# A hybrid decoder layer on one core: other queue, places and order for its recurrence (S5)

## The chip, the cores and the metric

One core of a Trainium2 chip runs the whole layer as one program. The metric is the device time of one execution in microseconds; the kernel before takes 786.01 us (median of three runs, 784.77 to 787.89).

## The reference

One layer of a decoder for 16 meta tokens and 512 prompt tokens in one sequence, and 8 sequences of 8 new tokens each with 1024 cached ones. The input is projected once to u, c_q, c_kv and k_r. u runs through a complex diagonal state space (S5: 32 groups of 16 channels and 64 states), the rest through latent attention with four heads. Their outputs share a projection, and a convolutional gated FFN follows. Cut to what the change touches:

```python
z = xn @ w_in;  u, c_q, c_kv, k_r = split(z, [512, 896, 1152])
abar, bbar = s5_discretise(a, log_dt, b)             # complex, per group
h[t] = abar * h[t-1] + bbar @ u[t]                   # associative scan over t
y = (re(h) @ c_re - im(h) @ c_im) + d * u
y = gelu(y);  y = y * sigmoid(y @ w_glu)
x = x + concat(y, mla) @ w_out
f = (silu(causal_conv(xn2 @ w_gate)) * (xn2 @ w_up)) @ w_down;  x = x + f
```

All outputs are float32: y, the latent cache rows, the final states and the last convolution rows.

## The kernel before, in words

The 592 tokens stand on the free axis, 128 features on the partitions. A product of two float32 matrices is made of three matmuls: both sides are split into a high part (ScalarE, L393) and a low part (VectorE, L394), and high x high, high x low and low x high are summed in PSUM (`mm3`). Small products of the recurrence run in plain float32, and such a matmul appears as two half passes.

SBUF is a set of banks A to J, one tile each; `R.get(name, shape, type, bank, at)` gives a place in a bank and `R.put` gives it back. The framework adds all waits from the accesses to those places, and plans the order of each engine's instructions from a timeline of its own: ready instructions in order of priority, which is the order in which the code emits them, moved forward by the numbers `p_...` and `f_...` of `KN` for the parts so named. Generators ("flows") yield amounts of planned time, so that their parts are emitted between the main line's.

**u and z.** `u_phase` forms u in four blocks (PSUM), scales it by `rxb` into `us`, both in bank D, stores each block to DRAM (`ud`, L638) and loads it back with the groups on other partitions (`U`, L639), all on SyncE's queue. `z_phase` forms c_q in three blocks; its evacuation copies the high part into `cqh`, at the beginning of bank D (as float32r, another type, so that the whole bank has to be free), takes the low part, and squares into `zacc` and `ztmp` (L675 to L676); GpSimd sums the squares (L678). Weights come through a ring of three buffers (`fill`, L237); the three blocks of c_kv's weights (`b_kv`) use that ring too.

**The recurrence.** Eight tokens form a chunk, so 74 chunks stand on the free axis. `w2_flow` prepares the matrices that turn a chunk of u into a state, four quarters in two buffers (VectorE L948 to L953, then transposes on TensorE). `taps_flow` prepares the chunk's own kernel: VectorE L1003 to L1008 fill `d3`, matmuls make the taps, and SyncE stores them as `kd` (L1020). Behind both, matmuls of W2 and U give the states `hb`, and eleven steps and a last one of four VectorE instructions each (`add_scaled`, L902 to L906) scan them over the chunks. In `hb` and `d3` the two groups of a pair lie on the two halves of the partitions, with real and imaginary part side by side. `swap` (three ScalarE copies of 64 partitions) exchanges halves, in `d3` for each quarter and in `hb` once, so that afterwards one group's real and imaginary parts fill 128 partitions.

**The output.** `s5_out_flow` loads T from `kd` (eight DMAs a quarter, L1046, two places in bank E for four quarters), and for each quarter and each parity runs a batch of four groups: T times U, then `d3` times `hb`, added in one PSUM bank (tag `bg`, one buffer). A copy to Y, a store (`yd`, L1066), four loads back (`ys`, L1073) and one gelu over all (L1075) follow. `glu` splits the result and multiplies it by the gate's weights. The flow starts at step 2 of `prompt_attn`, whose steps are 20 units of head and token block; the attention of the sampled tokens, the output projection and the FFN come behind the gate.

Names on the timelines are those of the banks: `bankD<-mmp` at L389 is the copy into `cqh`, `ud<-bankD` the store of u, `bgp` the PSUM bank of the recurrence, `krs` and `kr` the rotated keys, of which some matmuls use only 64 partitions.

Of the kernel before, what the change touches and what calls it, by code (L numbers as in the profile page):

```python
# [10 lines left out]
F32 = mybir.dt.float32  # L11
F32R = mybir.dt.float32r
I32 = mybir.dt.int32
AF = mybir.ActivationFunctionType
# [3 lines left out]
ADD, SUB, MUL = ALU.add, ALU.subtract, ALU.mult  # L18
AX = mybir.AxisListType.X

D = 1024
# [3 lines left out]
NT = NP + NS  # L25
S5W = 512
G = 32
P5 = 64
H5 = 16
# [10 lines left out]
LC = 8  # L40
NCP = NP // LC
NC = NT // LC
# [100 lines left out]
def dap(ap, off, dims):  # L143
# [4 lines left out]
KN = dict(bgb=1, chunks=(4, 6, 6, 6), cpo='0P1g2Wu34', cvo=0, endt=18.0, f_exp=24, f_s5=40, f_taps=28, gd=16,  # L148
          gdep=(2, 3), gord=(0, 1, 2, 3, 4), keyx=0, kre='pvvvp', lag=4, ldo='0P1g2W34W', mmb=4,
          order=(4, 3, 1, 2, 0), outs=2, outy=0.01, p_absorb=121, p_finT=-57, p_frows=126, p_inner2=243,  # L150
          p_innerT=-14, p_keys=26, p_pv=-261, p_qmm=25, p_qrope=-19, p_ropek=-199, p_scan=519, p_soft1=-22,
          p_ssoft=21, p_vals=-14, p_w0=98, warm=14, p_w1=78, p_w3=146, pfill=(1, 1, 2, 2, 3, 3), pre=(2, 3), pvd=(1, 1),
          rog='aaav', s2d=1, s5t=40.0, s5y=1.2, sume='pppp', swy=1.0, tapeng='vvvvvvvv',
          tapt=0, tapy=3.0, tpb=3, useng='vvpvppv', valx=4, w2q=((0, 2), (1, 3)), w2s=3.0, w2t=24.0, wsp=(2, 3),
# [139 lines left out]
class K:  # L294
# [124 lines left out]
    def weights(self):  # L419
        A, R, nc, v = self.A, self.R, self.nc, self.nc.vector  # L420
        one = lambda src: (lambda raw: [(raw, src)])
        items = []

        def add(src, shape, **kw):
            items.append(dict(src=src, shape=shape, **kw))

        def kv_split(k0, k1):
            def f(raw):
                self.split(raw, self.wc[:, 0, k0:k1], self.wc[:, 1, k0:k1])
            return f  # L430
        early = {3: ("C", 1024), 4: ("C", 0)}
        for j in range(7):
            add((lambda raw, j=j: [(raw[:, :4], A["b_in"][j][:, :4])]) if j < 2 else one(A["b_in"][j]), [8, 128])
            if j in early:
                items[-1]["at"] = early[j]
        for k0, k1 in ((0, 3), (3, 6), (6, 8)):
            add(one(A["b_kv"][:, k0:k1]), [k1 - k0, 320], split=kv_split(k0, k1))

        for j in range(6):
            add(one(A["b_uq"][j]), [3, 128])  # L440
        add(one(A["b_uk"]), [2, 512])
        add(one(A["b_uv"]), [2, 512])
        for m in range(4):
            add(one(A["b_glu"][m]), [4, 128])
        for m in (*KN["pre"], *range(8)):
            add(one(A["b_out"][m]), [8, 128])
        up = lambda nm, f: add(one(A[nm][f]), [8, 128])
        for c, (f0, f1) in enumerate(self.chunks):
            for f in range(f0, f1):
                if f == f0 == 0 or f > f0:  # L450
                    up("b_gate", f)
                up("b_up", f)
            if f1 < NF:
                up("b_gate", f1)
            for plan in self.plans(f1 == NF):
                self.add_down(add, items, A[f"b_down{c}"], (f1 - f0) // 2, plan)
        return Weights(self, items)
# [46 lines left out]
    def startup(self):  # L504
        nc, A, R, v, cp, p = self.nc, self.A, self.R, self.nc.vector, self.cpool, self.nc.gpsimd
        S = nc.sync
# [42 lines left out]
        ps = self.bg_ps()  # L549
# [2 lines left out]
        self.now = 5.0  # L552
        self.s5 = self.start(self.s5_flow(), pri="f_s5")
        self.step(self.s5)
        jk = R.get("junk", [512], F32, "D", 3472).bitcast(mybir.dt.bfloat16)
        for j in range(2):
            W.parts[j] = tuple(self.wtile(t, [8, 128]) for t in ("wh", "wl"))

# [57 lines left out]
    def u_phase(self):  # L616

        nc, A, R, v, S = self.nc, self.A, self.R, self.nc.vector, self.nc.sync
        W = self.W
        rxb = R.get("rxb", [NT], F32, "D", 2368)  # L620
        us = R.get("us", [4, LC, NC], F32, "D", 0)

        self.ud = self.dram.tile([4, LC, 128, NC], F32, name="ud")
        self.U = R.get("U", [G, NC], F32, "E", 3904)
        pm = self.pm = R.get("p1c", [KVR + 320], F32, "E", 0)
        S.dma_start(pm, A["c_p1"])
        self.gkv = pm[:, :KVR]
        self.rope = pm[:, KVR:].rearrange("p (i j) -> p i j", i=5)
        self.cmask = self.cpool.tile([128, 128], F32, name="cmask")
        self.smask = self.cpool.tile([128, 2, 64], F32, name="smask")  # L630

        def evac(m):
            ps = self.ups.pop(m)
            for o, a, b in UH:
                v.tensor_tensor(us[:, m, ::-1, a // LC:b // LC].rearrange("p s c -> p c s"),
                                ps[:, o, :b - a].rearrange("p (c s) -> p c s", s=LC),
                                rxb[:, a:b].rearrange("p (c s) -> p c s", s=LC), op=MUL)
            S.dma_start(self.ud[m].rearrange("s p c -> p s c"), us[:, m])  # L638
            S.dma_start(self.U[:, 8 * m:8 * m + 8].rearrange("p g c -> p (g c)"),  # L639
                        self.ud[m].rearrange("s (h g) c -> (s h) (g c)", g=8))  # L640
        self.u_part(2, 0, 5)
        pt = self.bg_ps()
        for i in range(4):
            self.T(pt[:, 128 * i:128 * i + 128], self.rx[:, i:i + 1].to_broadcast([128, 128]))
        self.copy(rxb[:, :512], pt)
        pt = self.bg_ps()
        self.T(pt[:, :128], self.rx[:, 4:5].to_broadcast([128, 128]))
        self.copy(rxb[:, 512:], pt[:, :NT - 512])
        W.split()
        self.u_part(2, 5, 8)  # L650
        evac(0)
        self.u_part(3, 0, 8, 0)
        evac(1)
        W.split()
        self.u_part(3, 0, 8, 1)
        evac(2)
        evac(3)
        self.loaded = True
        self.wc = R.get("wc", [2, 8, 320], F32R, "F", 0)
        R.put("us", "rxb")  # L660
# [107 lines left out]
    def s5_flow(self):  # L768
# [65 lines left out]

        b = self.bq
        bb = self.bb = R.get("bb", [2, NG, H5], F32, "E", 576)
        tb = R.get("tb", [2, NG, H5], F32, "D", 2960)
        fb = lambda r: f[:, r, :, None].to_broadcast([128, NG, H5])
        self.cmul(v, (bb[:, 0], bb[:, 1]), (fb(0), fb(1)), (b[:, 0], b[:, 1]), (tb[:, 0], tb[:, 1]))
        R.put("tb", "s5b")  # L840
# [70 lines left out]
            d = 1 << j  # L911
            add_scaled((3 * d, 66, 2 * d), (2 * d, 66 - d, 2 * d), j)
        add_scaled((74, 83, 1), (65, 74, 1), 0)
        self.scanned = True
        yield KN["endt"]
        hc = ts.rearrange("p g x r c -> p (g x r c)")[:, :256].rearrange("p (r b g) -> p r b g", r=2, b=8)
        self.copy(hc, hb[:, :, :, 75:83].rearrange("p g r b -> p r b g"))
# [9 lines left out]
        for r, n in enumerate(("o_re", "o_im")):  # L927
            nc.sync.dma_start(A[n + "_p"][0, 0].rearrange("(G a) p -> G (a p)", a=2), so[:16, 0, r])
            nc.sync.dma_start(A[n + "_s"][0].rearrange("b (G a) p -> (b G) (a p)", a=2), so[:, 1, r])
        yield KN["swy"]  # L930
        self.swap(hb[:, :, 0, :NC], hb[:, :, 1, :NC], ts.rearrange("p g x r c -> p (g x r c)")[:, :NG * NC].rearrange("p (g c) -> p g c", g=NG))
        R.put("scan")
        self.scan_done = True

    def w2_flow(self, eng, qs, at):

# [4 lines left out]
        for q in qs:  # L941
# [10 lines left out]
            eng.tensor_tensor(tmp[:, 1], pb[2], bc[2], op=MUL)  # L952
            self.w2i = eng.tensor_tensor(im, im, tmp[:, 1], op=SUB)  # L953
            yield 0.0
            while "x" in R.used:
                yield 0.5
            if "w2" not in R.used:
                self.w2t = R.get("w2", [4096], F32, "H", 0)
# [12 lines left out]
    def taps_flow(self):  # L971
# [5 lines left out]
        bd = R.get("bd", [2, 4, 2, H5], F32, "J", 0)  # L977
        v.memset(bd, 0.0)
        self.cs = R.get("s5cs", [16, H5], F32, "J", 256)
        v.tensor_tensor(self.cs, ct[:, 0], ct[:, 1], op=ADD)  # L980
        self.kd = self.dram.tile([H5, G, 240], F32, name="kd")
        zt = R.get("ztap", [112], F32, "J", 2240)
        v.memset(zt[:16], 0.0)
# [8 lines left out]
        for q in range(4):  # L992
# [7 lines left out]
            for i in range(2):  # L1000
                e = v if KN["tapeng"][2 * q + i] == "v" else p
                if i == 0:
                    e.tensor_tensor(dim, cb[0], pb[0], op=MUL)  # L1003
                e.tensor_tensor(tmp[:, i], cb[1 + i], pb[1 + i], op=MUL)
                if i == 0:
                    e.tensor_tensor(dre, dim, tmp[:, 0], op=SUB)
                else:
                    e.tensor_tensor(dim, tmp[:, 1], dim, op=SUB)  # L1008
# [10 lines left out]
            v.tensor_tensor(ksb[:, q, :H5], ksb[:, q, :H5], dm[:, q], op=ADD)  # L1019
            nc.sync.dma_start(self.kd.rearrange("h g m -> g h m")[8 * q:8 * q + 8, :, 112:], ksb[:, q])  # L1020
            yield 0.5
            x = tmp.rearrange("p i g k h -> p (i g k h)")[:, :512].rearrange("p (g k h) -> p g k h", g=4, k=8)
            self.swap(dre[:, :, 1:], dim[:, :, 1:], x)
            yield 0.5
        R.put("bd", "s5cs", "ztap", "dm", "ksb", "taptmp", "bb", "ct")
        self.taps_done = True

    def swap(self, a, b, t):

        self.copy(t[:64], b[:64])  # L1030
        self.copy(b[:64], a[64:])
        self.copy(a[64:], t[:64])

    def s5_out_flow(self):

# [6 lines left out]
        def load_T(q):  # L1042
            T[q] = R.get(f"T{q}", [8, LC, H5], F32, "E", 576 + 1024 * (q % 2))
            for s in range(LC):
                b = 16 * (LC - 1 - s)
                S.dma_start(T[q][b:b + 16].rearrange("h g t e -> h g (t e)"), self.kd[:, 8 * q:8 * q + 8, b:b + 128])  # L1046
        load_T(0)
        while not getattr(self, "scan_done", False):
            yield 0.5
# [3 lines left out]
        for q in range(4):  # L1053
            Y = R.get(f"Y{q}", [8, NC], F32, "E", 2624 + 592 * (q % 2))
            for a in range(2):
                ps = self.bg_ps()[:, :4 * NC].rearrange("p (g c) -> p g c", g=4)
                for j in range(4):
                    g = 8 * q + 2 * j + a
                    self.mm(ps[:, j], T[q][:, g % 8].rearrange("p t h -> p (t h)"), U[:, g], True, False)
                    self.mm(ps[:, j], d3[:, a, g // 2, 1:9].rearrange("p t h -> p (t h)"), hb[:, g // 2, a, :NC], False, True)  # L1060
                self.copy(Y[:, a:8:2], ps)
                yield KN["outy"]
            R.put(f"T{q}")
# [6 lines left out]
        ys = R.get("ys", [4, LC, NC], F32, "E", 0)  # L1070
        self.yg = R.get("yg", [4, NT], F32, "E", 2368)
        for m in range(4):
            self.ysd = S.dma_start(ys[:, m], self.yd[m].rearrange("t p c -> p t c"))  # L1073
        yield 8.0
        nc.scalar.activation(self.yg.rearrange("p m (c t) -> p m t c", t=LC), ys, AF.Gelu_apprx_tanh)  # L1075
        R.put("ys")
        self.gelu_done = True

# [920 lines left out]
```

## Time and profile before

| | us |
|---|---|
| median of three runs | 786.01 |
| the profiled execution | 791.1 |
| its span, first to last instruction | 789.3 |

| engine | busy us | share of the span |
|---|---|---|
| TensorE, matmuls (PE) | 742.7 | 94% |
| TensorE, weight loads (PEld) | 690.4 | 87% |
| VectorE (DVE) | 539.1 | 68% |
| ScalarE (ACT) | 351.3 | 45% |
| GpSimd (POOL) | 169.2 | 21% |

The mean granted clock of TensorE is 0.967 of 2.4 GHz. A row of a timeline gives the start and the length of one instruction (or of a run of like ones, x their number), counted from the span's start, and in brackets how long the engine had been idle before it and what ended that. Matmuls overlap in the pipeline, so the length of one is more than its share; the distance between two starts shows the pace. SPq and POOL rows with a DMA are the issue, not the transfer.

### The profile page before, as it was taken

To read this page: it belongs to the slowest core of one execution; us is meant where nothing else is said; L and a number is where in the kernel's file an instruction comes from. 1 tells how busy PE (TensorE), PEld (TensorE's weight loads), DVE (VectorE), ACT (ScalarE), POOL (GpSimd) and SP (SyncE) were. 2 spreads that over 40 slices of the span, in tenths; PEclk is the share of its full clock that TensorE was granted. 3 is DMA by queue.
4 is the path that set the end of the run, shared out by engine and by line. 5 is a ranking of instruction groups with operands and counts; after the bars stand their busy time and mean duration, and the time that the engine had idled before them with its cause. 6 is when DMAs were issued, how large, how long until landed. Compare 5 with 4: busy or idle time off the path is not lost.

```text
span 789.3 us, 14335 instructions
## 1 busy us (share of the span) xinstructions
PE 742.7 (94%) x5594; PEld 690.4 (87%) x5594; DVE 539.1 (68%) x1168; ACT 351.3 (45%) x661; POOL 169.2 (21%) x223
## 2 busy tenths in 40 slices
PE   9979978999879999999999999999999999999985
PEld 8979876778675567999999999999999999999885
DVE  7888999835335333644789566797666996667894
ACT  6435856666473312534334234343333432433643
POOL 0012021000220000331144011551111650114460
PEclk9989999779879999999999999999999999999998
DMA  9890331015694031332223322224222233322203
GB/s 338 239 172 25 97 98 47 6 44 153 197 347 164 1 133 52 108 102 74 67 54 114 121 79 77 61 61 154 66 95 68 61 94 106 99 76 88 52 22 120
DMA packets 41308, 81.49 MB, mean 103 GB/s; under 512 B 13380, under 2 KB 20468, under 8 KB 40216
## 3 DMA queue, kind: packets, MB, share of 16 engines
q1 hardware_dynamic: 39448, 70.09, 29.9%
q0 software_dynamic: 1792, 10.49, 3.6%
q8 instruction: 44, 0.72, 0.4%
q14 instruction: 24, 0.20, 0.1%
HBM read 74.18 MB, written 6.38 MB: 102 GB/s over the span
## 4 chain that ended last, share of the span: by engine, by line
PE 71%; DVE 14%; DMA 7%; ACT 5%; issue 2%; SPq 0%; DVEq 0%; ACTq 0%
PE mmp L379 57%; PE tpp L379 7%; DVE wl L394 4%; PE tpp L385 4%; PE bgp L379 4%; DMA ud<-bankD 1%; DMA bankC<-b_in 1%; DVE bankD L1784 1%; DMA bankF<-xrow 1%; DVE bankA L1736 1%; DMA wraw<-b_down 1%; ACT wh L393 1%; DMA wraw<-b_kv 1%; DMA bankG<-xT 1%; DVE bankC L394 1%
## 5 line engine op out<-in xcount | busy, mean ns | idle before, releaser
L379 PE MATMUL mmp<-bankF,wh 128*128 128x288 f32 (+1 forms) x768 | 224.1, 300 | 7.3 <-ACT bankF L393 7.0
L379 PE MATMUL mmp<-bankF,wl 128*128 128x288 f32 (+1 forms) x736 | 219.6, 299 | 0.2 <-DVE wl L394 0.2
L393 ACT ACTIVATE wh<-wraw 128x1024 fp32r<-128x1024 f32 (+3 forms) x103 | 85.4, 830 | 156.9 <-PE mmp L379 130.7
L379 PEld LDWEIGHTS mmp<-bankF,wh 128*128 128x128 f32 x768 | 146.0, 193 | 7.7 <-ACT bankF L393 7.2
L379 PEld LDWEIGHTS mmp<-bankF,wl 128*128 128x128 f32 x736 | 140.0, 190 | 0.4 <-DVE wl L394 0.4
L394 DVE TENSOR_TENSOR wl<-wraw,wh 128x1024 fp32r<-128x1024 f32 (+3 forms) x103 | 114.3, 1111 | 35.8 <-ACT wh L393 35.5
L379 PE MATMUL mmp<-bankH,wh 128*128 128x288 f32 (+1 forms) x440 | 130.5, 297 | 0.0
L379 PEld LDWEIGHTS mmp<-bankH,wh 128*128 128x128 f32 x440 | 83.7, 190 | 0.0
L379 PE MATMUL mmp<-bankB,wh 128*128 128x288 f32 (+2 forms) x324 | 76.3, 305 | 4.4 <-ACT wh L393 2.2
L379 PE MATMUL mmp<-bankJ,wh 128*128 128x288 f32 (+1 forms) x264 | 78.6, 298 | 0.0
L379 PEld LDWEIGHTS mmp<-bankB,wh 128*128 128x128 f32 x324 | 54.3, 191 | 7.7 <-ACT wh L393 3.1
L379 PE MATMUL mmp<-bankA,wh 128*128 128x290 f32 (+2 forms) x216 | 51.6, 303 | 5.6 <-ACT zacc L676 5.1
L379 PEld LDWEIGHTS mmp<-bankJ,wh 128*128 128x128 f32 x264 | 50.2, 190 | 0.0
L1749 POOL TENSOR_TENSOR bankA<-bankA,bankE 128x576 f32<-128x576 f32 x22 | 27.2, 1235 | 98.6 <-DVE bankA L1746 96.5
L1745 DVE TENSOR_TENSOR bankA<-bankA,mmp 128x288 f32<-128x288 f32 (+1 forms) x44 | 18.2, 420 | 42.8 <-PE mmp L379 28.7
L394 DVE TENSOR_TENSOR wl<-bankE,wh 128x384 fp32r<-128x384 f32 (+1 forms) x66 | 46.0, 715 | 0.0
L379 PE MATMUL mmp<-bankA,wl 128*128 128x290 f32 (+2 forms) x152 | 45.1, 302 | 0.0
L379 PEld LDWEIGHTS mmp<-bankA,wh 128*128 128x128 f32 x216 | 37.2, 192 | 7.0 <-ACT zacc L676 5.4
L393 ACT ACTIVATE wh<-bankE 128x384 fp32r<-128x384 f32 (+1 forms) x66 | 30.3, 486 | 15.1 <-PE mmp L379 5.8
L379 PE MATMUL mmp<-bankB,wl 128*128 128x288 f32 (+1 forms) x118 | 35.3, 299 | 1.6 <-DVE wl L394 1.6
L1738 ACT ACTIVATE bankA<-bankA 128x592 f32<-128x592 f32 x22 | 15.4, 700 | 47.3 <-DVE bankA L1737 47.3
L379 PE MATMUL mmp<-bankG,wh 128*128 128x288 f32 x150 | 34.3, 295 | 0.0
(425 smaller groups left out, 1672.7 us busy)
## 6 DMA issues: line engine op xcount, KB each, us to landing
wraw<-b_gate SPq DMA_DIRECT2D x22, 512.0 KB, 3.4
wraw<-b_up SPq DMA_DIRECT2D x22, 512.0 KB, 3.4
wraw<-b_down SPq DMA_DIRECT2D x17, 384.0 KB, 3.0
wraw<-b_out SPq DMA_DIRECT2D x10, 512.0 KB, 3.6
bankF<-xrow SPq DMA_DIRECT2D x5, 512.0 KB, 7.8
bankA<-b_down SPq DMA_DIRECT2D x6, 384.0 KB, 3.1
bankE<-kd SPq DMA_DIRECT2D x32, 64.0 KB, 2.2
bankG<-xT SPq DMA_DIRECT2D x6, 296.0 KB, 4.8
```

What stands on the lines that cost most here:

```text
L379: self.nc.tensor.matmul(out, lhsT, rhs, start=start, stop=stop, **kw)
L385: self.nc.tensor.transpose(out, src, self.ident[:n, :n])
L393: nc.scalar.activation(hi, src, AF.Copy)
L394: nc.vector.tensor_tensor(lo, src, hi, op=SUB)
L1736: v.scalar_tensor_tensor(c[:, :m], g[:, 1:NG - 1], self.gcol("cw1", f), c[:, :m], op0=MUL, op1=ADD)
L1738: nc.scalar.activation(s[:, :m], c[:, :m], AF.Silu)
L1745: v.tensor_tensor(c[:, a:a + n], s[:, a:a + n], pu[:, o, :n], op=MUL)
L1749: nc.gpsimd.tensor_tensor(c[:, :NU], c[:, :NU], self.rfb[:, 2:], op=MUL)
L1784: v.tensor_tensor(x, ps, x, op=ADD)
```

## The change

c_kv's weights get places of their own in bank H instead of the ring's; `rxb` moves to H, `us` to G (where x was), two small scratch tiles move from D to E, so that bank D holds c_q alone. The loads of U, T and ys are issued by GpSimd instead of SyncE. W2's transposes are emitted behind z, and the taps' VectorE work is ordered behind W2's. `swap` is gone: the output multiplies the real and the imaginary part in two matmuls of 64 partitions each. The output flow gets a priority of 150, no longer waits for the states' store and the exchange to be emitted, and its gelu runs in four blocks.

```diff
-KN = dict(... p_scan=519, p_soft1=-22,
+KN = dict(... p_scan=519, f_out=150, p_soft1=-22,
...
-            add(one(A["b_kv"][:, k0:k1]), [k1 - k0, 320], split=kv_split(k0, k1))
+            add(one(A["b_kv"][:, k0:k1]), [k1 - k0, 320], split=kv_split(k0, k1), at=("H", 592 + 320 * k0))
...
-        jk = R.get("junk", [512], F32, "D", 3472).bitcast(mybir.dt.bfloat16)
+        jk = R.get("junk", [512], F32, "E", 1760).bitcast(mybir.dt.bfloat16)
...
-        rxb = R.get("rxb", [NT], F32, "D", 2368)
-        us = R.get("us", [4, LC, NC], F32, "D", 0)
+        rxb = R.get("rxb", [NT], F32, "H", 0)
+        us = R.get("us", [4, LC, NC], F32, "G", 256)
...
-            S.dma_start(self.U[:, 8 * m:8 * m + 8].rearrange("p g c -> p (g c)"),
+            nc.gpsimd.dma_start(self.U[:, 8 * m:8 * m + 8].rearrange("p g c -> p (g c)"),
...
-        tb = R.get("tb", [2, NG, H5], F32, "D", 2960)
+        tb = R.get("tb", [2, NG, H5], F32, "E", 1760)
...
-        self.scanned = True
+        self.scan_done = True
         yield KN["endt"]
...
-        yield KN["swy"]
-        self.swap(hb[:, :, 0, :NC], hb[:, :, 1, :NC], ts.rearrange("p g x r c -> p (g x r c)")[:, :NG * NC].rearrange("p (g c) -> p g c", g=NG))
         R.put("scan")
-        self.scan_done = True
...
-            while "x" in R.used:
+            while "x" in R.used or not hasattr(self, "fq"):
...
-        v.tensor_tensor(self.cs, ct[:, 0], ct[:, 1], op=ADD)
+        self.after(v.tensor_tensor(self.cs, ct[:, 0], ct[:, 1], op=ADD), self.w2i)
...
-                e.tensor_tensor(tmp[:, i], cb[1 + i], pb[1 + i], op=MUL)
+                self.after(e.tensor_tensor(tmp[:, i], cb[1 + i], pb[1 + i], op=MUL), self.w2i)
...
-            x = tmp.rearrange("p i g k h -> p (i g k h)")[:, :512].rearrange("p (g k h) -> p g k h", g=4, k=8)
-            self.swap(dre[:, :, 1:], dim[:, :, 1:], x)
-            yield 0.5
...
-                S.dma_start(T[q][b:b + 16].rearrange("h g t e -> h g (t e)"), self.kd[:, 8 * q:8 * q + 8, b:b + 128])
+                nc.gpsimd.dma_start(T[q][b:b + 16].rearrange("h g t e -> h g (t e)"), self.kd[:, 8 * q:8 * q + 8, b:b + 128])
...
                     self.mm(ps[:, j], T[q][:, g % 8].rearrange("p t h -> p (t h)"), U[:, g], True, False)
-                    self.mm(ps[:, j], d3[:, a, g // 2, 1:9].rearrange("p t h -> p (t h)"), hb[:, g // 2, a, :NC], False, True)
+                    h = slice(64 * a, 64 * a + 64)
+                    for r in range(2):
+                        self.mm(ps[:, j], d3[h, r, g // 2, 1:9].rearrange("p t h -> p (t h)"), hb[h, g // 2, r, :NC], False, r == 1)
...
-            self.ysd = S.dma_start(ys[:, m], self.yd[m].rearrange("t p c -> p t c"))
+            self.ysd = nc.gpsimd.dma_start(ys[:, m], self.yd[m].rearrange("t p c -> p t c"))
         yield 8.0
-        nc.scalar.activation(self.yg.rearrange("p m (c t) -> p m t c", t=LC), ys, AF.Gelu_apprx_tanh)
+        for m in range(4):
+            nc.scalar.activation(self.yg[:, m].rearrange("p (c t) -> p t c", t=LC), ys[:, m], AF.Gelu_apprx_tanh)
```

## Rows read from the trace of the kernel before

**Rows 1.** Stages: length, then per engine busy us (instructions); PEclk; DMA share; GB/s.

```profile
30.00:49.00 19.00, 19.00 (x142) 18.56 (x140) 17.92 (x34) 4.10 (x7) 0.00 (x0) 1.00 0.96 127
54.10:57.70 3.60, 3.60 (x15) 3.60 (x16) 3.47 (x6) 1.46 (x4) 2.56 (x1) 0.50 0.42 114
57.70:97.50 39.80, 39.80 (x413) 36.39 (x412) 33.58 (x104) 25.98 (x74) 5.06 (x8) 1.00 0.24 64
97.50:153.00 55.50, 45.16 (x267) 38.15 (x268) 54.31 (x166) 31.65 (x83) 9.46 (x18) 0.88 0.19 53
153.00:174.00 21.00, 18.95 (x101) 15.38 (x100) 9.42 (x38) 16.50 (x43) 0.00 (x0) 0.76 0.19 45
174.00:215.20 41.20, 39.26 (x294) 33.55 (x292) 17.90 (x64) 20.19 (x61) 5.71 (x6) 0.95 0.59 168
222.20:228.30 6.10, 6.10 (x25) 6.10 (x26) 2.78 (x4) 2.92 (x4) 1.94 (x2) 0.50 1.02 426
```

**Rows 2.** TensorE's waits: what waited, for whom, us in total, times, longest.

```profile
PE mmp L379 <- ACT bankF L393: 7.0, 1, 7.0
PE mmp L379 <- ACT zacc L676: 5.1, 1, 5.1
```

**Rows 3.** Timeline, ScalarE at 49 us: start, us, engine, line, operation [idle before].

```profile
49.22 1.29 ACT L389 ACTIVATE bankD<-mmp,small 128x290 fp32r<-128x290 f32 x3 [5.95 <-DMA ud<-bankD]
```

**Rows 4.** Chain of waits, 159 to 162.5 us: start, us, what.

```profile
159.28 1.10 ACT bankE L389
...
161.45 1.21 ACT bankG L389
```

**Rows 5.** VectorE, taps' L1004 grouped (busy, mean ns); timeline, scan's first and last.

```profile
L1004 DVE TENSOR_TENSOR bankJ<-bankE,s5psd 128x576 f32<-128x576 f32 x6 | 4.5, 754 | 0.5 <-ACT bankG L389 0.5
...
89.33 1.22 DVE L902 TENSOR_TENSOR bankE<-bankG,s5ca 128x1024 f32<-128x1024 f32 x1
...
152.35 0.44 DVE L906 TENSOR_TENSOR bankG<-bankG,bankE 128x288 f32<-128x288 f32 x1
```

**Rows 6.** ScalarE, one of three groups of the taps' exchange.

```profile
L389 ACT ACTIVATE bankG<-bankG 64x512 f32<-64x512 f32 x4 | 2.5, 630 | 3.7 <-PE bgp L379 3.7
```

**Rows 7.** Timeline, TensorE from 186 us.

```profile
186.08 0.60 PE L379 MATMUL mmp<-bankB,bankJ 128*98 128x264 f32 x3
186.53 0.28 PE L379 MATMUL mmp<-krs,bankF 128*98 128x264 f32 x1
186.74 0.36 PE L379 MATMUL mmp<-kr,bankF 64*98 64x264 f32 x1
187.03 0.58 PE L385 MATMUL tpp<-ident,bankH 104*128 104x104 f32 x4
187.44 0.36 PE L379 MATMUL bgp<-bankE 128*128 128x74 f32 x2
...
189.17 0.62 PE L379 MATMUL mmp<-bankB,bankJ 128*104 128x430 f32 x2
```

**Rows 8.** Timeline, SyncE's DMA issues, then GpSimd.

```profile
49.13 0.32 SPq L639 DMA_DIRECT2D bankE<-ud  x1
...
176.56 3.62 SPq L1046 DMA_DIRECT2D bankE<-kd  x8
...
55.14 2.98 POOL L678 TENSOR_TENSOR zacc<-zacc,ztmp 128x290 f32<-128x290 f32 x1 [5.46 <-ACT ztmp L676]
...
129.39 1.16 POOL L1185 DMA_INDIRECT bankH<-cache_kr,idx  x1 [8.50 <-PE mmp L379]
...
217.18 0.94 POOL L1187 DMA_INDIRECT bankD<-cache_ckv,idx  x1 [0.30 <-issue]
218.43 0.95 POOL L1185 DMA_INDIRECT bankC<-cache_kr,idx  x1 [0.31 <-issue]
```

**Rows 9.** Timeline, ScalarE from 215 us.

```profile
215.65 1.28 ACT L1075 ACT_TABLE_LOAD   x1
216.94 4.45 ACT L1075 ACTIVATE bankE<-bankE 128x2368 f32<-128x2368 f32 x1
```

More of the change, by code (lines that the diff above doesn't have):

```diff
@@ L150 @@
           order=(4, 3, 1, 2, 0), outs=2, outy=0.01, p_absorb=121, p_finT=-57, p_frows=126, p_inner2=243,
-          p_innerT=-14, p_keys=26, p_pv=-261, p_qmm=25, p_qrope=-19, p_ropek=-199, p_scan=519, p_soft1=-22,
+          p_innerT=-14, p_keys=26, p_pv=-261, p_qmm=25, p_qrope=-19, p_ropek=-199, p_scan=519, f_out=150, p_soft1=-22,
           p_ssoft=21, p_vals=-14, p_w0=98, warm=14, p_w1=78, p_w3=146, pfill=(1, 1, 2, 2, 3, 3), pre=(2, 3), pvd=(1, 1),
@@ L1021, in taps_flow @@
             yield 0.5
-            x = tmp.rearrange("p i g k h -> p (i g k h)")[:, :512].rearrange("p (g k h) -> p g k h", g=4, k=8)
-            self.swap(dre[:, :, 1:], dim[:, :, 1:], x)
-            yield 0.5
         R.put("bd", "s5cs", "ztap", "dm", "ksb", "taptmp", "bb", "ct")
         self.taps_done = True
[L1028 to L1032, printed above, removed]
     def s5_out_flow(self):
```

## The prediction

> **What bounds the kernel now.** I read the page's slices first, then a table by stages, then the waits of TensorE, the chain of waits, and the timelines around each gap. From 320 us on nothing that is edited runs, so all of the change lies in the first 222 us, and there the stages have different limits [rows 1]. Up to 49 us TensorE is packed: 142 matmuls in 19.00 us, 0.134 us each. It then stands still for 5.1 us, and the 15 matmuls after that take 3.60 us, 0.24 each, at granted clock 0.50 (1.2 GHz). From 57.7 to 97.5 TensorE is full again. From 97.5 to 153 VectorE is the limit: 54.31 of 55.50 us busy, with TensorE at 45.16 and clock 0.88. After 153 VectorE is half idle and TensorE is nearly full, 18.95 of 21.00 and 39.26 of 41.20 us, but partly at the lower clock (0.76, 0.95). Last comes a gap of 7.0 us before the gate, and 6.10 us of matmuls at 0.50 behind it [rows 1, 2].
>
> Two of TensorE's waits are worth having: 5.1 us on the square that empties z's PSUM bank, and 7.0 us on the first split of the gated y [rows 2]. The first is a place conflict. ScalarE's copy into bank D sat idle for 5.95 us until the store of u, which lies in the same words, had been read out [rows 3].
>
> **The change part by part.**
>
> *Own places for u, its scale and c_kv's weights.* z's copies then wait for no DMA: 5.1 us of stall go, and with them the half rate of 15 matmuls, 15 x (0.24 - 0.134) = 1.6 us, if the clock then holds. Together 6.7 us, the upper end. TensorE alone does not decide it: VectorE must do the same work in a shorter stretch. Over 30 to 49, 54.1 to 57.7 and 57.7 to 97.5 it is idle 1.1 + 0.1 + 6.2 = 7.4 us [rows 1], so there is room, just.
>
> *Taps behind W2.* W2's third and fourth quarters reuse the buffers of the first two and wait for TensorE's transposes of those. So far taps fill such holes: six of L1004 alone are 4.5 us [rows 5]. Now they may not, and the transposes are issued only behind z. Bounds for the first two edits together: 6.7 - 4.5 = 2.2 to 6.7 us; I take **-5**, nearer the upper end, because the DMA stall is certain and the holes are not all long. Nothing is added to VectorE. The scan, which ran from 89.33 to 152.8 [rows 5], starts sooner: by those 5 us and by the taps of two blocks that no longer stand before it, ten operations of 0.75 us (L1004's duration), 7.5 us. I put its end at about 140.
>
> *No exchange of state halves.* Three ScalarE copies behind the scan go; two of them are pieces of the chain, 1.10 and 1.21 us [rows 4]. The three copies in each of four taps blocks go too, 4 x 3 x 0.63 = 7.6 us (one of three such groups is in [rows 6]), but beside ScalarE's 31.65 of 55.50 us that is off the path. Gain 0 to 3.6; I take **-2.3**. The T loads and the first output batch need no longer wait for the exchange.
>
> The price is on TensorE. The output runs in eight batches of four groups. Each group had two matmuls of 128 partitions and now has one of 128 and two of 64. Sixteen half passes, eight matmuls, took from 187.44 to 189.17, 0.22 us each [rows 7], so 64 cost 14.1 and 96 cost 21.1: **+7.0** as the lower bound. The rows with a 64-partition matmul say more. With 264 columns the step from the 128-partition one to it is 0.21 us and from it to the next 0.29, where three full ones beside them take 0.15 each [rows 7]. That is some 0.06 to 0.14 extra at each change of height, at 64 changes 4 to 9 us, so +7 to **+16** in all. (The Trainium skill, TensorE: Matmul & The Clock Gate, section LDWEIGHTS, says that a weight load takes time by its columns and not by its partitions, so half the height is no cheaper. That speaks against the change and gives the 7.0; the rows give more.)
>
> Where does this land? Before 153 TensorE idles 10.3 of 55.5 us [rows 1], and what runs there is free. With the scan ended at 140, three of the eight batches (2.6 to 3.8 us each) can run under the VectorE limit, none of which did before save one matmul. So of +7 to +16, some 8 to 11 is covered: net -4 to +8. I take **+3**, nearer the lower price plus some of the changes.
>
> *Loads on GpSimd's queue.* 40 DMAs leave SyncE's queue: 4 of U, 32 of T, 4 of ys. On SyncE eight T loads issue in 3.62 us; GpSimd's own DMAs follow each other at 1.25 us, busy 0.94 [rows 8], so eight cost about 10 us: +6.4 us a block. The first two blocks lie beside the scan and cost nothing. The third and fourth wait until their place is given back, and follow one another. If the output starts at 140, three blocks of 10, two last batches of 3 and as much for y's way through DRAM (an estimate) make 42 us, and it still ends before attention does, at 215; without that cover the two exposed blocks cost some 2 x 6. Behind the waiting U loads on GpSimd stand z's sums (L678), behind T's loads rope's sums (L1231) and the gathers; ScalarE's ztmp and the query splits wait for those. For U I take 0 to 2 us, at 0, since its last load was issued at 49.13 and the first sum ran at 55.14 [rows 8]. SyncE loses the waits for u's store, so c_kv's weights come early.
>
> (The Trainium skill, DMA: Bandwidth & Descriptors, section SWDGE vs HWDGE vs iDMA, says that GpSimd writes descriptors in software into SBUF, where VectorE can lock it out, and that SyncE's path is free of this. The trace agrees weakly.) Amid a VectorE that hardly paused, GpSimd's DMA took 1.16 us, against 0.94 [rows 8].
>
> *Gelu by blocks, output sooner.* Today table load, 4.45 us of gelu and the first split follow the last attention split in series [rows 9], and TensorE waits 7.0. If y is back before attention ends, only a split is left: -6. If it is late, the last block is a quarter, and 4.45 x 3/4 = 3.3 still go. The matmuls behind it, 25 in 6.10 us, 0.24 each, would take 3.4 at full clock: another -2.7, at worst 0 [rows 1]. I take **-8.7**. A gelu amid the exponentials costs ScalarE a table load of 1.28 [rows 9] each way, up to eight; in 174 to 215.2 it is busy 20.19 of 41.20 us, so I put that at nothing; uncovered it is 1.3 to 10.
>
> *Clock after 153.* With fewer holes TensorE may keep 2.4 GHz in 153 to 174. There 0.76 means up to 21 x 0.24 = 5.0 us; I take **-2** of 0 to 5.
>
> Sum: -5 - 2.3 + 3 - 8.7 - 2 = **-15.0**. The profiled execution took 791.1 (span 789.3, 1.8 around it) and would take 776.1. It lies 5.1 above the median of 786.0, so I predict 771. Bounds by term: 2.2 + 0 - 8 + 3.3 + 0 = 2.5 faster at worst, 6.7 + 3.6 + 4 + 8.7 + 5 = 28 at best: 758 to 783.5.
>
> **Rivals.**
>
> *A, all of the output hides.* If the scan ends near 125, six or more batches run under the VectorE limit and the tail from 153 to 215 loses its 14.1 us of them. For it: W2, now unbroken, feeds the scan, whose own operations are only about half of what VectorE does from 89 to 153. Against: the same share of other work will stand between them. In place of the +3 stands -10: -28, 758.
>
> *B, the time moves along.* VectorE's total from 30 to 153 is unchanged, its holes go to the transposes, and the dearer matmuls eat the gelu gap: -2.2 - 2.3 + 8 - 6 = -2.5, 783.5, up to 786.
>
> *C, slower: GpSimd's queue sets TensorE's pace.* The output is raised by 150 in the ordering, and TensorE runs in order: where its matmuls stand before attention's and T's third and fourth blocks are not there, TensorE waits. Price: 2 x 6 us of issue, 2 x 2 of landing and 2 x 1.6 of half clock, 19, with all 16 us of dearer matmuls open. Against them stand the gains that remain, 5 + 2.3 + 8.7 = 16: +19, 805. With one of the two blocks exposed it is 16 + 9.5 - 16 = +9.5, which I take: 795.5. Rope's sums, held behind a block of loads, could add up to 10. It decides from the point where stalls and open matmuls together exceed 16 us. For it: eight loads of 10 us behind each other. Against: the order is planned with some price for these DMAs, and the gathers before show no such stall.
>
> *D, it doesn't do what it says:* another holder of bank D, so that z waits still. I see none in the places; 0.03, 778.
>
> **How the numbers follow.** Forecast 0.45, A 0.25, B 0.14, C 0.13, D 0.03. Less than 0.5% (4 us) is about what a measurement of this kernel can tell from no change. Faster by over 0.5%: A, D and nearly all of the forecast and some of B, 0.74; within: most of B and a rest, 0.12; slower: C and a rest, 0.14. Range 755 to 790: A's end with its bounds, B whole, and the nearer part of C.
>
> **What would show it.** Right: no wait of TensorE for zacc at 49, clock 1.00 through 60; the first L902 near 76; the first bgp of the output near 140; no gelu in front of the gate; and no 64x1184 copies. The matmul price shows in the step from a 128- to a 64-partition one. Wrong: gaps of TensorE that end on a DMA into bank E, a longer stretch from 153 to the gate, or VectorE idle at 50 to 58 for transposes.

## The result and the profile after

The changed kernel took 827.45 us (median), the kernel before 785.98: a ratio of 1.0513, 95% interval 1.0468 to 1.0559, 41 us slower where 15 us faster was forecast, and outside the range of 755 to 790. The profiled execution has a span of 826.7 us. The gate, told by the load of its activation table, comes at 260.7 us instead of 223.9, and from there on the two traces run alike (566.0 and 565.5 us to the end). Of the 37 us before it, 5.6 lie ahead of the scan's end (158.4 against 152.8); the other 31 lie between the scan's end and the gate.

First the table by stages of the kernel after: stretch, length, busy time and instructions of PE, PEld, DVE, ACT, POOL, then the granted clock, DMA share and GB/s.

```profile
49.00:54.10 5.10, 5.10 (x40) 5.10 (x40) 5.05 (x10) 1.83 (x5) 3.93 (x3) 1.00 0.44 126
...
86.20:158.50 72.30, 60.10 (x375) 51.16 (x371) 68.54 (x214) 43.17 (x115) 13.57 (x26) 0.85 0.19 55
...
158.50:186.00 27.50, 26.96 (x144) 22.31 (x144) 10.28 (x34) 12.98 (x39) 10.38 (x18) 0.75 0.27 70
186.00:208.50 22.50, 22.50 (x79) 18.14 (x79) 5.39 (x21) 5.76 (x17) 4.28 (x8) 0.50 0.24 78
208.50:244.00 35.50, 35.50 (x147) 30.71 (x146) 4.63 (x17) 9.19 (x23) 3.72 (x4) 0.55 0.15 42
244.00:263.00 19.00, 17.37 (x76) 13.89 (x76) 6.43 (x15) 10.17 (x18) 7.62 (x8) 0.50 0.57 184
```

The 5.1 us in which TensorE stood still are filled: 5.10 of 5.10 busy, clock 1.00, where [rows 2] had the wait. But from 186 to 244 TensorE has no hole at all, 58.0 of 58.0 us busy, and the granted clock is 0.50 to 0.55 (1.2 GHz for all of it but 208.4 to 211.8). Before, the last six batches of the output ran at 0.95 [rows 1]. So in this stretch TensorE isn't waiting; it runs at half rate.

The chain of waits shows the output's batches one by one: start, length, what.

```profile
166.35 3.67 PE bgp L379 x24
173.63 3.67 PE bgp L379 x24
186.19 6.80 PE bgp L379 x24
196.05 6.54 PE bgp L379 x24
209.08 4.36 PE bgp L379 x24
218.05 6.63 PE bgp L379 x24
226.90 6.54 PE bgp L379 x24
237.65 6.50 PE bgp L379 x24
```

A batch of 24 half passes (12 matmuls) takes 3.67 us at 2.4 GHz, where one of 16 took 1.73 [rows 7]; behind the second batch the clock falls, and a batch takes 6.5 to 6.8 (the fifth, in part at full clock, 4.36). Together they take 44.7 us. The 64-partition matmuls of the first batch use partitions 0 to 63 and those of the second 64 to 127, and both batches take 3.67 us, so it does not matter which half it is.

### The profile page after: what moved, and what is told of

Read it like the earlier page. It is cut to its first block, busy times and chain, and to the rows that moved or that the text cites. A ratio compares the mean times of both kernels' runs of the same rounds, so it can differ in the third digit from the quotient of the medians.

```text
span 826.7 us, 14450 instructions
## 1 busy us (share of the span) xinstructions
PE 791.8 (96%) x5658; PEld 728.3 (88%) x5658; DVE 538.6 (65%) x1168; ACT 344.1 (42%) x649; POOL 194.4 (24%) x263
## 4 chain that ended last, share of the span: by engine, by line
PE 76%; DVE 14%; issue 3%; ACT 3%; DMA 3%; POOL 0%; DVEq 0%; SPq 0%; ACTq 0%
PE mmp L379 58%; PE tpp L379 7%; PE bgp L379 7%; PE tpp L385 5%; DVE wl L394 4%; DMA bankG<-cache_ckv,idx 1%; DVE bankD L1775 1%; DVE bankA L1727 1%; DMA wraw<-b_down 1%; ACT wh L393 1%; DVE bankE L903 1%; DVE bankC L394 1%; DVE bankG L906 0%; DVE bankE L902 0%; DMA bankG<-xT 0%
## 5 line engine op out<-in xcount | busy, mean ns | idle before, releaser
L393 ACT ACTIVATE wh<-wraw 128x1024 fp32r<-128x1024 f32 (+3 forms) x103 | 85.4, 830 | 158.4 <-PE mmp L379 131.5
L379 PE MATMUL bgp<-bankG 64*128 64x74 f32 (+1 forms) x156 | 37.3, 391 | 1.0 <-POOL bankG L508 1.0
L379 PEld LDWEIGHTS bgp<-bankG 64*128 64x128 f32 (+1 forms) x156 | 31.2, 285 | 4.7 <-POOL bankG L508 1.0
```

What stands on the lines that cost most here:

```text
L379: self.nc.tensor.matmul(out, lhsT, rhs, start=start, stop=stop, **kw)
L393: nc.scalar.activation(hi, src, AF.Copy)
```

## The experiments

Theory H (height, the number of partitions that a matmul uses): the 64-partition matmuls cost more and bring the low clock. Rival O: the raised order of the output does. Rival C: GpSimd's queue does.

**Full height, exchange put back.**

```
-  h = slice(64 * a, 64 * a + 64)
-  for r in range(2):
-      self.mm(ps[:, j], d3[h, r, ...], hb[h, g // 2, r, :NC], False, r == 1)
+  self.mm(ps[:, j], d3[:, a, ...], hb[:, g // 2, a, :NC], False, True)
+  (self.swap(...) behind each taps block and behind the scan, and the output's start behind that, as before)
```

> The changed kernel with the exchange of the state halves and of the taps' halves put back, so that the output has 64 matmuls of 128 partitions instead of 32 of 128 and 64 of 64... counted per group, 2 matmuls instead of 3; all else as changed. Theory H (half height): eight batches shrink from 3.67 us at full clock to about 1.73, 15.5 us, and the granted clock, which stood at 0.50 from 177.7 to 208.4 and from 211.8 to 263, stays at 1.00 for most of that stretch, some 25 us more: 827 to about 786, between 780 and 792. Rival O (order): the output, raised by 150, cuts attention into pieces that keep TensorE at the low clock whatever the matmuls' height: only the 15.5 us come back, 811 to 813, and the clock stays at 0.50 in two long stretches.

803.0 us, ratio 1.020 (1.017 to 1.023). The two long stretches at 0.50 (177.7 to 208.4 and 211.8 to 263) are gone, against rival O: the clock is 1.00 from 167 to 210, and 0.50 again from 211 to 228, beside the waits for the gate. But 11 us more than H's upper end remain. The timeline of GpSimd and SyncE shows them, in y's way through DRAM:

```profile
210.09 0.32 SPq L1065 DMA_DIRECT2D yd<-bankE  x1
...
221.27 0.94 POOL L1187 DMA_INDIRECT bankD<-cache_ckv,idx  x1 [5.26 <-PE mmp L379]
222.51 0.94 POOL L1187 DMA_INDIRECT bankD<-cache_ckv,idx  x1 [0.30 <-issue]
223.44 0.95 POOL L1072 DMA_DIRECT2D bankE<-yd  x1
```

The last store of y is issued at 210.09, its load at 223.44: on GpSimd's queue two gathers stand ahead of it, and they wait for TensorE.

**Half height alone, in the kernel before** (the loop above, without the exchange; nothing else).

> The kernel before with one edit: no exchange of halves, the output's state part as two 64-partition matmuls a group. Theory H: 786 - 2 + 15.5 + 15 to 28 of clock, 815 to 827, with long stretches at granted clock 0.50 behind the first batches. Rival O: 786 - 2 + 15.5 = about 799, clock as before (0.95 in the stretch of the last six batches).

830.5 us, 1.055 (1.048 to 1.061); the granted clock in its output stretch (163 to 241) is 0.62. This one edit costs at least as much as the whole change (826.9 and 834.0 in two runs, where the whole change took 822.7 to 828.4); H, and a little more than its upper end.

**Three matmuls a group, all of 128 partitions** (`d3[:, r, ...]`, `hb[:, g // 2, r, :NC]` in the changed loop).

> The changed kernel with the two 64-partition matmuls of each group run over all 128 partitions instead (so each group's output adds up both halves, which is not the reference's; the count of matmuls, their columns and their order are unchanged). It tells height from number. If height sets both price and clock: batches of about 2.6 us (12 matmuls at 0.22), clock back at 1.00, 827 - 8.5 - 25 = about 793. If number and order set them: 3.67 us a batch, clock at 0.50 as in the changed kernel, 825 to 830.

789.1 us, 1.002 (1.000 to 1.004). Chain of waits, the first and third batch, then its stages:

```profile
164.71 2.64 PE bgp L379 x24
...
178.75 2.83 PE bgp L379 x24
```

```profile
158.50:186.00 27.50, 26.84 (x207) 23.73 (x207) 13.10 (x48) 15.98 (x49) 11.27 (x19) 0.98 0.34 103
186.00:208.50 22.50, 21.75 (x176) 19.98 (x174) 7.81 (x27) 13.30 (x33) 9.73 (x14) 1.00 0.42 110
```

The same number of matmuls of the same columns in the same loop order, over 128 partitions instead of 64: clock 0.98 and 1.00, a batch mostly 2.65 instead of 3.67, and 38.4 us less. This is the decisive run: height sets both. How it sets the clock, the run doesn't say.

**Loads back on SyncE** (`nc.gpsimd.dma_start` to `nc.sync.dma_start` for U, T and y).

> The changed kernel with the loads of U, T and y issued by SyncE again. Theory H: nothing, 825 to 830, since no gap of TensorE ends on one of these loads. Rival C of the prediction (GpSimd's queue sets the pace): 10 to 19 us come back, 808 to 818.

825.0 us; its 822.2 to 827.8 overlap the changed kernel's 822.7 to 828.4. Rival C falls for this kernel, as H had it. With full height and the exchange back it is another matter:

**Full height, exchange, and SyncE's loads** (the first experiment and this one together).

> The changed kernel with the exchange of halves and full-height matmuls put back, and the loads of U, T and y on SyncE's queue. With the loads on GpSimd's queue this kernel took 803: the last load of y was issued at 223.44, 13.4 us after y's last quarter had been stored (210.09), behind two gathers of the cache (221.27 and 222.51) that stood ahead of it on GpSimd's queue, and TensorE waited 4.2 us. Theory Q (queue): the load follows its store at once and the gate comes some 10 us sooner: 790 to 796. Rival X: the exchange itself, which lies between the scan's end (157.1) and the second batch of the output (175.7), sets the end: 799 to 804.

793.1 us, 1.008 (1.005 to 1.010), 9.9 less than with GpSimd's queue: theory Q. The gate comes at 218.0 instead of 233.3. The exchange still lies between the scan's end at 157.3 and the first product with the states, at 175.8. Timeline of ScalarE:

```profile
167.93 1.21 ACT L389 ACTIVATE bankE<-bankG 64x1184 f32<-64x1184 f32 x1
...
169.78 1.21 ACT L389 ACTIVATE bankG<-bankG 64x1184 f32<-64x1184 f32 x1
...
172.36 1.20 ACT L389 ACTIVATE bankG<-bankE 64x1184 f32<-64x1184 f32 x1
```

**Own places alone, in the kernel before.**

```
+ b_kv: at=("H", 592 + 320 * k0);  us "D",0 -> "G",256;  rxb "D",2368 -> "H",0
+ junk, tb -> "E",1760;  W2's buffer taken once fq exists
```

> The kernel before with the own places alone (u, its scale, c_kv's weights, and the two small tiles that had to move with them, and W2's buffer claimed one step later); exchange, loads, taps and gelu as before. Prediction's first term: the 5.1 us wait at 49 goes and 2.2 to 6.7 us are won, 779 to 784. Rival B (the time moves along): TensorE is 5 us earlier at 49, and the stretch where VectorE is the limit is as much longer, 785 to 788.

792.4 us, 1.006 (1.004 to 1.009): not won, but lost, and more than rival B had. Its stages:

```profile
49.00:60.00 11.00, 11.00 (x75) 9.38 (x74) 11.00 (x20) 3.97 (x9) 4.37 (x4) 1.00 0.24 81
97.50:153.00 55.50, 44.03 (x232) 37.48 (x232) 52.30 (x154) 29.14 (x75) 6.75 (x16) 0.75 0.16 47
```

The stall at 49 is gone, as forecast, but VectorE is now busy for all of the 11.00 us from 49 to 60, and nothing is left of the gain at the scan's end: its last operation starts at 153.3, where it started at 152.35 [rows 5]. TensorE's clock from 97.5 to 153 is 0.75 where it was 0.88 [rows 1]; whether that is a cause or a result, the trace doesn't say.

**Fewer changes of height** (every second group's three matmuls in the opposite order).

> The changed kernel with every second group's three matmuls in the opposite order, so that a batch changes between 128 and 64 partitions 4 times instead of 7. If the price lies in the change of height (0.06 to 0.14 us by the prediction), a batch at full clock takes 3.67 - 3 x 0.1 = about 3.4 and less at the low clock: 820 to 825. If it lies in the 64-partition matmul itself, batches stay at 3.7 to 3.8 and 6.7: 825 to 830, with the clock at 0.50 as long as before.

818.1 us, 1.039 (1.034 to 1.044), below the range of either theory. Its chain of waits has the first batch and a slow one at

```profile
167.77 3.23 PE bgp L379 x24
...
189.23 5.91 PE bgp L379 x24
```

so three changes of height fewer save 0.44 of the 1.02 us that half height costs a batch, 0.15 each. Seven changes at 0.15 are the whole 1.02. The timelines of TensorE say the same; first the changed kernel, then three full matmuls a group, then this run:

```profile
166.46 0.66 PE L379 MATMUL bgp<-bankG 64*128 64x74 f32 x4
167.06 0.44 PE L379 MATMUL bgp<-bankE 128*128 128x74 f32 x2
167.43 0.66 PE L379 MATMUL bgp<-bankG 64*128 64x74 f32 x4
```

```profile
164.72 0.61 PE L379 MATMUL bgp<-bankG 128*128 128x74 f32 x4
165.17 0.39 PE L379 MATMUL bgp<-bankE 128*128 128x74 f32 x2
165.39 0.61 PE L379 MATMUL bgp<-bankG 128*128 128x74 f32 x4
```

```profile
167.87 1.11 PE L379 MATMUL bgp<-bankG 64*128 64x74 f32 x8
168.91 0.67 PE L379 MATMUL bgp<-bankE 128*128 128x74 f32 x4
```

Four half passes of 64 partitions take 0.60 us from start to start, and the two of 128 behind them 0.37; with all of them at 128 it is 0.45 and 0.22. Each run of either height is 0.15 longer, and eight of 64 in a row take 1.04, twice 0.45 and one time 0.14. So the price stands at the change of height, in both directions, and not on the 64-partition matmul. The clock falls here too, at the end of the third batch instead of behind the second, and is at 0.50 from 186.3 to 230.7.

**Own places and taps behind W2, in the kernel before** (two `self.after(..., self.w2i)` more).

> The kernel before with the own places and the taps ordered behind W2. Prediction's first two edits together: -2.2 to -6.7, 779 to 784, the first scan operation near 76 and the last near 140. Rival B: scan end within 3 us of 152.8 and 785 to 789. If the order of the taps alone costs, it is slower than the run with the places alone.

790.4 us, 1.005 (1.003 to 1.006). This is above rival B's range as well. VectorE's last scan line, grouped (count, ns, first and last start): the scan ends 4 us later than in [rows 5], not 13 earlier.

```profile
L906 DVE TENSOR_TENSOR bankG<-bankG,bankE x12: 206/494/1215, 94.1 to 156.3; 128x1024 f32<-128x1024 f32 x2, 128x32 f32<-128x32 f32 x2, 128x512 f32<-128x512 f32 x1, 128x256 f32<-128x256 f32 x1
```

**The kernel before, a second trace.**

> The kernel before once more, for a second trace: the profiled execution that the prediction reads lay 5.1 us above the median. If the 5 us are the low clock in 153 to 228, this trace shows a shorter stretch at 0.50 there and the gate before 223.9; if not, they lie behind the gate. Time 785 to 788.

785.2 us, span 783.4. The row that answers to 153 to 174 in [rows 1]:

```profile
153.00:174.00 21.00, 19.05 (x139) 16.24 (x138) 9.60 (x38) 16.14 (x45) 0.00 (x0) 1.00 0.24 61
```

The low clock in this stretch (0.76) belonged to that execution and not to the kernel. Here the gate comes at 218.5, not 223.9, and the last scan operation ends at 151.4.

**Gelu in blocks alone, in the kernel before.**

> The kernel before with gelu in four blocks, nothing else. Prediction's fifth term: the gap before the gate falls from 7.0 us to about 1 and the half-clock matmuls behind it go, 776 to 781. Theory N (next bound): the gate comes 3 to 6 us sooner, but the sample's cache gathers, which run at 320 to 390 GB/s around it, are what the next stretch waits for, and 0 to 3 us arrive at the end: 783 to 788.

788.3 us, 1.003 (1.001 to 1.005), a little above theory N's range. Its timeline, TensorE's last matmul of attention and GpSimd's gathers:

```profile
215.11 0.94 POOL L1188 DMA_INDIRECT bankE<-cache_ckv,idx  x1 [0.31 <-issue]
220.65 0.42 PE L379 MATMUL mmp<-bankD,bankB 16*128 16x98 f32 x2
221.84 0.94 POOL L1188 DMA_INDIRECT bankD<-cache_ckv,idx  x1 [5.79 <-issue]
```

The same place in the second trace of the kernel before:

```profile
209.12 0.66 PE L379 MATMUL mmp<-bankD,bankB 16*128 16x98 f32 x2
210.54 0.94 POOL L1187 DMA_INDIRECT bankD<-cache_ckv,idx  x1 [4.65 <-PE mmp L379]
```

So with gelu in blocks the gate does come 6.5 us sooner, at 212.0, but its matmuls pass attention's last ones (from 209.1 to 220.7), and the two gathers into bank D, which need their place, go from 210.5 to 221.8. The FFN starts 3.6 us later, at 348.7 against 345.1.

**Full height, no exchange, SyncE's loads.**

> The changed kernel with full-height matmuls, two a group, and SyncE's loads, but with the exchange of halves still left out (in the scan's states and in the taps, so each of these matmuls meets one right and one wrong half and the output is not the reference's). Against the run with the exchange put back (793.1) it prices the exchange. Prediction's second term: 0 to 3.6 us cheaper, 789 to 793. Rival X (the exchange lies on the path from the scan's end to the second batch, where 8 us passed): 5 to 9 us cheaper, 784 to 788.

785.2 us, 1.000 (0.997 to 1.002): 7.9 us less than with the exchange (6.4 by the ratios of the two to the kernel before): rival X's 5 to 9. Its first batch starts at 166.2 and takes 1.74 us.

**Gelu in blocks and the output raised by 150.**

> The kernel before with gelu in four blocks and the output raised by 150 in the order, the two edits that can bring the gate forward without touching the matmuls, the places or the queues. If the output's batches are held back by their rank, the last one ends 3 to 6 us before 206 and the time falls to 778 to 783. If they are held by the scan's end and by T's loads, it does the same as gelu in blocks alone, within 2 us.

787.2 us, 1.002 (1.000 to 1.004), as gelu alone within 2 us: the rank isn't what holds the output.

**Gelu in blocks, with the order kept** (the gate's first matmuls ordered behind attention's, the later gathers behind the first two); then the same with the output raised.

> The kernel before with gelu in four blocks, and the gate's first matmuls and the later cache gathers put behind attention's last matmuls and the first two gathers, as they stood before. With gelu in blocks alone the gate came 6.5 us sooner (211.97 against 218.47), but its matmuls had passed attention's last ones (at 220.7 instead of 209.1), and the two gathers into bank D, which wait for those, were issued at 221.8 instead of 210.5. Theory P (passing): the gathers are issued near 210 again, TensorE's waits at 231 to 235 go, and 3 to 6 us are kept: 780 to 784. Rival D (DMA): the gathers move 390 GB/s around the gate anyway and end where they ended, so nothing is kept: 785 to 789.

> The run with gelu in blocks and the gate held behind attention, and the output raised by 150 as well. The rank alone changed nothing that could be told (787.2 against 788.3): the same here, within 2 us of the held run, 780 to 784 by theory P, 785 to 789 by rival D.

785.2 and 784.8 us, ratios 0.999 (0.997 to 1.000) and 0.999 (0.997 to 1.002): not to be told from the kernel before, and nearer to rival D than to theory P. The gate comes at 213.8, the gathers into bank D at

```profile
214.06 0.94 POOL L1191 DMA_INDIRECT bankD<-cache_ckv,idx  x1 [6.79 <-DVE bankF L397]
215.31 0.94 POOL L1191 DMA_INDIRECT bankD<-cache_ckv,idx  x1 [0.30 <-issue]
```

and TensorE waits for other gathers later, 1.6 us at 228 and 1.1 at 232. Of 4.7 us won at the gate 1.5 reach the FFN in the trace (343.6 against 345.1). Passing was a part, the gathers themselves the rest; how the rest divides between bandwidth and order stays open. No version tried beats the kernel before by more than a measurement can tell.

**Half height in two of four blocks.**

> The changed kernel with 64-partition matmuls in the output's first two blocks (four batches) and 128-partition ones in the last two (whose groups add up both halves, so the output is not the reference's). It tells whether the low clock follows the height, batch for batch. Theory H: low clock in and behind the third and fourth batch, 1.00 from some way into the fifth, half of the 38 us that the full height gave back: 803 to 813. Rival: a low clock that, once there, lasts to the gate whatever runs: 818 to 826.

811.1 us, 1.031 (1.025 to 1.038), in theory H's range. Its stages, cut where the clock changes:

```profile
158.00:176.30 18.30, 17.68 (x113) 14.74 (x113) 6.80 (x27) 9.22 (x28) 4.98 (x10) 0.97 0.19 52
176.30:207.00 30.70, 30.70 (x116) 24.95 (x115) 9.72 (x33) 9.78 (x30) 9.68 (x17) 0.50 0.28 89
207.00:224.10 17.10, 17.10 (x149) 16.59 (x149) 4.51 (x17) 8.63 (x23) 3.74 (x5) 1.00 0.27 76
```

The clock falls behind the second half-height batch, stays at 0.50 through the third and fourth, and is back at 1.00 at 207.0. The first full-height batch starts only at 207.6, so that batch isn't what brought it back: the clock rose near the end of 6.5 us of attention matmuls. At the same place it rose in the changed kernel too, and fell again within the half-height batch that started at 209.08:

```profile
208.40:211.80 3.40, 3.40 (x25) 2.94 (x23) 0.00 (x0) 0.63 (x2) 0.92 (x1) 1.00 0.17 28
```

With full-height batches behind it, it stays. So the low clock isn't a state that lasts to the gate; it comes back with half-height batches.

## Why the prediction was wrong, point by point

**The clock** is the term that failed, with its sign: -2 was put down, for fewer holes. Full height instead of half gives back 38.4 us (827.5 - 789.1); 8 x (3.67 - 2.65) = 8.2 of them are the matmuls at full clock, and the other 30, by difference, are the half rate, of the batches and of the attention, transposes and gate between and behind them. The prediction took the low clock for a result of TensorE's gaps, because before it stood beside gaps [rows 1, 2], and so asked only whether holes would grow. None of its rivals held this; the slower one, C, was a matter of a queue. Where it looked at 64-partition rows, it asked for their length alone. What in the half-height batches takes the clock down stays open: it may be the partitions that stand empty or the stops at the changes of height. No run has the one without the other; with fewer changes the clock fell one batch later.

**The matmuls' price** at full clock was bounded at +7 to +16 and is 8 x (3.67 - 1.75) = 15.4, near the upper end: 7.2 for the third matmul of a group (2.65 - 1.75 a batch, 1.75 as in the kernels with two), 8.2 for half height. Per change of height 0.15 us was measured, the upper bound being 0.14, so this reading of [rows 7] was right in kind and nearly in size. What failed is the +3 that was chosen from it, because three batches were to run under VectorE's limit. None did: the first one starts at 166. (The Trainium skill, TensorE: Matmul & The Clock Gate, section LDWEIGHTS, has a weight load take time by its columns alone. The trace agrees: in the changed kernel's first two batches the median weight load of 64 partitions takes 187 ns, that of 128 takes 189. The price of half height is at the changes.)

**Own places and taps behind W2**, -5: measured +3.5 us, with the places alone +5.4. The step that fails isn't the stall, which goes as told; it is that VectorE has room for the same work in a shorter stretch and that nothing is added to it. With the places alone it is busy 11.00 of 11.00 us from 49 to 60. The scan starts 3 us sooner in the changed kernel (86.3 instead of 89.3), not 13, and ends 6 us later, at 158.4. VectorE was busy 68.54 us between; in the second trace of before the scan took 63.2 us, with 62.07 busy. More of attention's softmax now stands between its operations. VectorE's groups by line over the scan, after, then the second trace of before:

```profile
L1338 DVE TENSOR_REDUCE ast<-mmp 98x1 f32<-98x264 f32 (+4 forms) x14 | 5.9, 424 | 0.6 <-PE mmp L379 0.6
L394 DVE TENSOR_TENSOR bankD<-tpp,bankD 128x392 fp32r<-128x392 f32 (+7 forms) x12 | 4.0, 358 | 0.0
```

```profile
L1347 DVE TENSOR_REDUCE ast<-mmp 98x1 f32<-98x264 f32 (+4 forms) x10 | 4.2, 454 | 0.0
L394 DVE TENSOR_TENSOR bankD<-tpp,bankD 128x392 fp32r<-128x392 f32 (+7 forms) x8 | 2.4, 356 | 0.0
```

Four row maxima and four splits of probabilities more stand before the scan's end, 3.3 of the 6.5 us by which VectorE is busier. Rival B's name fits, the time moved along, but B had VectorE's total unchanged. Why the places alone come out 5 us slower stays open; the trace shows the lower clock, 0.75, and the gate at 223.0, where the second trace of the kernel before has 218.5.

**No exchange**, -2.3: mis-sized. In the changed kernel's surroundings it is worth 7.9 us (793.1 against 785.2), since not the copies' 3.6 us but the whole way from the scan's end to the first product with the states hangs on them: ScalarE does them between softmax work, from 167.9 to 173.6. In the kernel before they lie from 159.3 to 162.7 [rows 4]; what they cost there was not measured.

**GpSimd's queue**, 0: right in its sum for this kernel (SyncE's loads are 2.5 us faster, with overlapping times), wrong in its terms. A load of T takes 0.53 us there in a row of eight, and one of y 0.95, not the 1.25 that was taken from the gathers; eight of T take

```profile
87.04 4.22 POOL L1034 DMA_DIRECT2D bankE<-kd  x8 [13.05 <-ACT bankJ L389]
```

against 3.62 on SyncE [rows 8]. The danger was elsewhere: y's load stands behind gathers that wait. With full height the gate came at 233.3 by it, and at 218.0 with SyncE's loads; 9.9 us of that reached the end.

**Gelu by blocks**, -8.7: the gap before the gate goes, and the gate comes 6.5 us sooner, near the forecast's 6. At the end it is +2 us, for the sample's gathers are the next bound. The prediction stopped its chain at the gate and didn't ask who needs the place that attention's last matmuls hold.

**The profile against its median**: 5.1 us were carried over as a constant. They were the low clock from 163.5 to 173.7 in that execution, the same stretch from which the -2 was to be gained.

**The bounds**: the sum of the worst terms, 2.2 + 0 - 8 + 3.3 + 0, is -2.5, which means 2.5 us slower and not "2.5 faster at worst". The upper bound should have been 788.5, not 783.5; the stated range covers both.

The terms measured one by one do not add up exactly: without the height, the change is 1.5 us (by its own ratio) to 3 us (by the medians) slower than before, while its parts give 7.2 + 3.5 - 7.9 + 2.2 = +5, and perhaps 2.5 for the queue.

## What to carry to other kernels

Halving a matmul's partitions to save a copy is to be tried alone and first: it costs time at every change of height and, in a stretch full of such matmuls, the clock of everything around them. Follow a gain past the next engine: here 5 us at z were gone by the end of VectorE's stretch, and 6.5 at the gate came to nothing behind matmuls that overtook others and gathers that waited for their place. A load moved to a queue stands behind whatever waits there.

## What the runs showed of the hardware

TensorE without a hole, 58.0 of 58.0 us busy, was granted 1.2 GHz for all but 3.4 us of them, behind two batches with 64-partition matmuls, and 2.4 GHz (0.98 and 1.00) with the same number of matmuls over 128 partitions. The clock rose in a stretch of attention matmuls between the batches, at 208.4 in the changed kernel and at 207.0 with half height in two blocks of four. Within the next half-height batch it fell again, at 211.8; with full-height batches it stayed.

A weight load of 64 partitions took as long as one of 128 (187 and 189 ns), and eight half passes of 64 in a row took no longer than eight of 128 but for 0.14 us. Each change between the heights cost 0.15 us, seven in a batch: 3.67 against 2.65 us.

GpSimd issued a load of y 13.4 us after the store of its data (210.09 to 223.44), behind two gathers that waited for TensorE; SyncE issued it 2.3 us after the store (208.59 to 210.93).
